# The shift and scale vectors of an adaLN layer: made block by block, or two row blocks in one run

## The chip, the cores and the metric

The kernel runs on one core of a Trainium2 chip. The metric is the time of one execution on the device in microseconds (us). The five engines of the core that matter here are TensorE (PE; its weight loads are shown as PEld), VectorE (DVE), ScalarE (ACT), GpSimd (POOL) and SyncE (SP), whose queue issues nearly all transfers.

## What is computed

One layer of a hybrid diffusion backbone on 640 tokens (128 of context, 512 latent) of width 1024. Each row is normalised and modulated, goes through one wide input projection into attention, a gated linear recurrence and Fourier mixing, and comes back through one output projection. Only the head of the layer is touched by the change:

```
mod_ctx = silu(c_ctx) @ w_ada + b_ada          # context tokens
mod_lat = silu(c) @ w_ada + b_ada              # latent tokens
shift, scale, gate = split(mod, 3)
h = rmsnorm(x, g_pre) * (1 + scale) + shift
proj = h @ w_in
```

`w_ada` is 1024 x 3072 in fp32, so the two thirds that make shift and scale are 8 MB. The latent and the context tokens have vectors of their own, so each entry is needed for two conditions.

## The kernel before

The 1024 channels are cut into KT = 8 row blocks of 128. Tokens lie on the free axis after a transpose: `hT[0]` and `hT[1]` (the high and the low part of h, 128 x 8 x 640 each) are the operands of every input projection. A projection is three matmuls for each block k, each half u of 320 tokens (`mm3`, line 208: high x high, high x low, low x high).

**The loading phase** is `start_stream` (line 242). It issues the loads of x, then for each k two 128 x 1024 blocks of weights (`wss`, 512 KB each, scale and shift of the 128 channels of block k), EARLY = 3 blocks ahead, and for the first two k also a block of `win`. The loads stand in one chain on SP's queue. All x tiles are multiplied by their 1/rms in `scale_x`. Then, for each k:

- `mod_cols` (line 192) makes a raw vector: eight matmuls for each of the two weight blocks, in four groups of 32 output partitions that are added up later. They write two quarters of a PSUM buffer `pm`.
- VectorE copies the 128 x 256 partial sums into `row` (line 264), PE transposes them back into `pm` (line 268), VectorE sums the four groups (line 270) and makes G = (sum + bias + 1) * g_pre in two instructions (lines 271, 272) and the shift in one (line 273).
- `modulated` (line 231): PE transposes four x tiles of block k into a PSUM buffer `px` and the context tile into the last quarter of `pm`; ScalarE makes h from them with G as scale and the shift as bias (line 235 for the 512 latent tokens, line 237 for the 128 of context); VectorE cuts h into `hT[0]` and `hT[1]` (lines 238, 239).

As soon as h of a block is there, `zf_stream` (line 281) adds 12 matmuls of the first two projection blocks to four accumulators `zf_acc` (line 206), which it holds for the whole phase; behind it `fill` (line 956) brings the next projection, `zb0`, from the event "h4" on. After the last block ScalarE runs `gate` (line 319) on the four accumulators, and these come free.

**What sets the order.** `Order` (line 39) runs the streams as generators with rough due times (`od.now`, `LAT`), and so fixes the order in which instructions are written. A planner then goes through them with times of its own and lays down the queue of every engine: an instruction that was written earlier goes first when it is ready by the planner's times. On the chip each queue is worked off in that order. PSUM has eight buffers: five of tag "b" and three of tag "f" (`WB`, line 27). `zf_acc` takes three "f" and one "b"; `pm`, `px` and the first half of `zb0` take "b"; the second half of `zb0` takes an "f".

Of the kernel before, what the change touches and what calls it, by code (L numbers as in the profile page):

```python
# [9 lines left out]
F32 = mybir.dt.float32  # L10
F32R = mybir.dt.float32r
U32 = mybir.dt.uint32
ACT = mybir.ActivationFunctionType
ALU = mybir.AluOpType
AX = mybir.AxisListType
PSUM = bass.MemoryType.PSUM

P = 128
D = 1024
KT = 8  # L20
NT = 640
# [7 lines left out]
EARLY = 3  # L29
# [42 lines left out]
def mixer_kernel(ctx: ExitStack, tc: tile.TileContext, A, O):  # L72
    nc = tc.nc
    sc, ve, gp, te, sy = nc.scalar, nc.vector, nc.gpsimd, nc.tensor, nc.sync
# [5 lines left out]
    sp = ctx.enter_context(tc.tile_pool(name="sp", bufs=WB["s"]))  # L80
    ps = ctx.enter_context(tc.tile_pool(name="ps", bufs=8, space=PSUM))

    od = Order()
# [3 lines left out]
    def nm(s):  # L87
        n_[0] += 1
        return f"{s}_{n_[0]}"

    def T(cols=NT, dt=F32, tag=""):
        return tp.tile([P, NT], dt, tag="t", name=nm("t" + tag))[:, :cols]

    def PE_():
        return tp.tile([P, 512], F32, tag="pe", name=nm("pe"), bufs=WB["pe"])

    def S(cols):
        if cols <= 16:
            return sp.tile([P, 16], F32, tag="s", name=nm("s"))[:, :cols]
        return sp.tile([P, 320], F32, tag="m", name=nm("m"), bufs=WB["m"])[:, :cols]  # L100
# [4 lines left out]
    def PB(tag="b"):  # L105
        return ps.tile([P, 512], F32, tag=tag, name=nm("pb"), bufs=WB["p" + tag])
# [3 lines left out]
    def mm(out, lhsT, rhs, start=True, stop=True):  # L110
        n, m = rhs.free_size(), lhsT.free_size()
        od.now += 1e-3 * (n * 0.4167 * 4 if rhs.dtype == F32 else max(n * 0.4167, m * 0.83)) + 2e-3
        return te.matmul(out, lhsT, rhs, start=start, stop=stop).ins  # L113

    def follow(chain, ins):

        if chain:
            tc.add_manual_dep(ins, chain[-1].name, mybir.DependencyInfo(mybir.DependencyClass.NoSync,
                                                                        mybir.DependencyReason.DATA), reason="turns")
        chain.append(ins)  # L120

    def tr(out, src):
        od.now += 0.107
        last_tr[0] = te.transpose(out, src, ident).ins  # L124

    def split(src, hi, lo, hi_eng=None, lo_eng=None):
        (sc.copy if hi_eng is None else hi_eng.tensor_copy)(hi, src)  # L127
        (ve if lo_eng is None else lo_eng).tensor_sub(lo, src, hi.bitcast(F32))  # L128
# [5 lines left out]
    def const(name, shape, dt=F32, dma=gp.dma_start):  # L134
        t = cp.tile([P, *shape], dt, tag=name, name=name)
        if name in A:
            dma(t, A[name])
        return t
# [3 lines left out]
    bss = const("bss", [KT, 2])  # L142
    gpre = const("gpre", [KT])
# [22 lines left out]
    csil = const("csil", [KT, 32])  # L166
# [5 lines left out]
    def load_raw(src, tag, shape=(KT, P)):  # L172
        t = (tp if tag == "vs" else wp).tile([P, *shape], F32, tag=tag, name=nm(tag), bufs=WB[tag])
        with tc.issue_after(wdma[-1]) if wdma else ExitStack():
            wdma.append(sy.dma_start(t, src).ins)
        return t

    def split_w(raw, lo_eng=None, shape=(KT, P), tags=("hi", "lo")):
        hi, lo = [wp.tile([P, *shape], F32R, tag=t, name=nm(t), bufs=WB[t]) for t in tags]
        split(raw, hi, lo, lo_eng=lo_eng)  # L180
        return hi, lo
# [7 lines left out]
        with tc.issue_after(wdma[-1]) if wdma else ExitStack():  # L189
            sy.dma_start(t, src)  # L190

    def mod_cols(out, w):

        t = od.now
        for k in range(KT):
            o = out[32 * (k % 4):32 * (k % 4) + 32, :]
            mm(o, csil[:, k, :], w[:, k, :], start=(k < 4), stop=(k >= 4))
        od.now = t + 0.45

    shift, G, rstd = const("shift", [KT, 2]), const("G", [KT, 2]), const("rstd", [5])  # L200
    hT = [big.tile([P, KT, NT], F32R, tag=f"hT{j}", name=f"hT{j}") for j in range(2)]
    xa, xb = [T(tag="xa") for _ in range(5)], [T(384, tag="xb") for _ in range(5)]

    def xcols(i, k):
        return (xa[i] if k < 5 else xb[i])[:, k % 5 * P:k % 5 * P + P]
    zf_w, zf_acc = [], [[PB("f"), PB("f")], [PB("f"), PB()]]
# [8 lines left out]
    def load_x():  # L215
        for i in range(5):
            load(xa[i], A["x"][i * P:(i + 1) * P, 0:NT])
            load(xb[i], A["x"][i * P:(i + 1) * P, NT:D])

    def scale_x():  # L220
        for i in range(5):
            ss2 = S(2)
            sc.activation(T(), xa[i], ACT.Square, accum_out=ss2[:, 0:1])
            ve.tensor_tensor_reduce(PE_()[:, 0:384], xb[i], xb[i], 1.0, 0.0, op0=ALU.mult, op1=ALU.add,
                                    accum_out=ss2[:, 1:2])
            ve.tensor_add(rstd[:, i:i + 1], ss2[:, 0:1], ss2[:, 1:2])
            rsqrt_mean(rstd[:, i:i + 1], D)
            ve.tensor_scalar(xa[i], xa[i], rstd[:, i:i + 1], 0.0, op0=ALU.mult, op1=ALU.add)
            ve.tensor_scalar(xb[i], xb[i], rstd[:, i:i + 1], 0.0, op0=ALU.mult, op1=ALU.add)

    def modulated(k, pm):
        h, px = T(), PB()
        for i in range(1, 5):
            tr(px[:, (i - 1) * P:i * P], xcols(i, k))
        sc.activation(h[:, P:NT], px, ACT.Identity, bias=shift[:, k, 1:2], scale=G[:, k, 1:2])
        tr(pm[:, 384:512], xcols(0, k))
        sc.activation(h[:, 0:P], pm[:, 384:512], ACT.Identity, bias=shift[:, k, 0:1], scale=G[:, k, 0:1])
        ve.tensor_copy(hT[0][:, k, :], h)
        ve.tensor_sub(hT[1][:, k, :], h, hT[0][:, k, :].bitcast(F32))
        od.set(f"h{k}", LAT["h"])  # L240

    def start_stream():
        load_x()
        raws, zraw = [], []

        def loads(k):
            for u in range(2):
                raws.append(load_raw(A["wss"][2 * k + u], RAW[2 * k + u]))
            if k < 2:
                zraw.append(load_raw(A["win"][k], "raw"))  # L250

        for k in range(EARLY):
            loads(k)
        scale_x()
        od.now = 11.0
        for k in range(KT):
            if k + EARLY < KT:
                loads(k + EARLY)
            row = sp.tile([P, 256], F32, tag="AC", name=nm("row"), bufs=2)
            pm = PB()  # L260
            for u in range(2):
                mod_cols(pm[:, u * P:(u + 1) * P], raws[2 * k + u])
            yield 0
            ve.tensor_copy(row, pm[:, 0:256])
            yield LAT["row"]

            for u in range(2):
                tr(pm[:, u * P:(u + 1) * P], row[:, u * P:(u + 1) * P])
            pt = S(4)
            ve.reduce_sum(pt, pm[:, 0:256].rearrange("p (u g r) -> p u r g", u=2, r=32)[:, :, 0:2, :], axis=AX.X)  # L270
            ve.tensor_scalar(G[:, k, :], pt[:, 0:2], bss[:, k, 0:1], 1.0, op0=ALU.add, op1=ALU.add)
            ve.tensor_scalar_mul(G[:, k, :], G[:, k, :], gpre[:, k:k + 1])  # L272
            ve.tensor_scalar_add(shift[:, k, :], pt[:, 2:4], bss[:, k, 1:2])
            modulated(k, pm)
            if k < 2:
                zf_w.append(split_w(zraw[k]))
            if k == 1:
                od.set("zw", 0.0)
            yield max(0.0, 13.5 + 2.7 * (k + 1) - od.now)

    def zf_stream():
        yield "zw"
# [9 lines left out]
        od.set("zf", 0.0)  # L292

    od.add(start_stream())
    od.add(zf_stream())

# [832 lines left out]
```

## Time and profile before

| | us |
|---|---|
| median of three runs | 436.22 (436.12 to 437.0) |
| the profiled execution | 437.11 |
| its span, from the first to the last instruction | 435.3 |
| PE busy | 411.3 |
| VectorE busy | 303.5 |
| ScalarE busy | 205.8 |

The busy time of PE has the ends of its matmuls modelled, so a busy PE is not one at its peak: the time from one start to the next is what counts. The chain of waits is followed back from the last instruction: at each step to what released it, or to the instruction before it on its engine. All times in the rows below count from the start of the span.

### The profile page before, as it was taken

How to read it: one execution, taken by the hardware profiler on the slowest of the kernel's cores; microseconds unless marked ns; L12 is line 12 of the kernel's file. 1: busy time of each engine (PE TensorE's matmuls, PEld its weight loads, DVE VectorE, ACT ScalarE, POOL GpSimd, SP SyncE). 2: the span in 40 equal slices, each digit the busy share in tenths (PEclk: the TensorE clock that was granted, in tenths of full speed). 3: DMA queues.
4: the chain of work that ended last, by engine and by line, in shares of the span. 5: the costliest groups of instructions: out<-in, count | busy, mean ns of one | idle time of the engine just before them, and what ended most of it. 6: DMA issues, size and time to landing. Idle time of an engine off the chain costs nothing.

```text
span 435.3 us, 8309 instructions
## 1 busy us (share of the span) xinstructions
PE 411.3 (94%) x3176; PEld 372.7 (86%) x3176; DVE 303.5 (70%) x866; ACT 205.8 (47%) x546; POOL 7.4 (2%) x23
## 2 busy tenths in 40 slices
PE   0699999999998999999999999999999999999994
PEld 0488899999988998999899889889898988988884
DVE  2775479999986866885597658885768928670174
ACT  6434467565341526654444444753556643350161
POOL 2000000000020100000000000000000000000000
PEclk9999999999999999999999999999999999999998
DMA  7996153211302021122021413245134302481023
GB/s 236 412 407 229 49 158 114 74 45 50 88 20 76 10 62 48 56 97 74 32 68 60 145 50 104 98 147 163 51 119 150 96 0 66 140 291 48 0 105 139
DMA packets 19528, 47.62 MB, mean 109 GB/s; under 512 B 3184, under 2 KB 6912, under 8 KB 19488
## 3 DMA queue, kind: packets, MB, share of 16 engines
q1 hardware_dynamic: 19376, 46.94, 32.0%
q8 instruction: 25, 0.41, 0.4%
q0 software_dynamic: 112, 0.14, 0.3%
q14 instruction: 15, 0.12, 0.1%
HBM read 43.80 MB, written 3.28 MB: 108 GB/s over the span
## 4 chain that ended last, share of the span: by engine, by line
PE 90%; DVE 3%; DMA 3%; ACT 1%; issue 1%; SPq 0%; DVEq 0%; ACTq 0%
PE pb L113 84%; PE pb L124 7%; DMA vs<-wss 2%; DMA txa<-x 1%; DVE AL L450 1%; DVE t L524 1%; DVE AL L487 0%; ACT L679 0%; DVE t L951 0%; ACT pe L680 0%; DVE t L467 0%; DVE t L466 0%; DVE AC L450 0%; DVE t L468 0%; SPq L190 0%
## 5 line engine op out<-in xcount | busy, mean ns | idle before, releaser
L113 PE MATMUL pb<-hT,hi 128*128 128x320 f32 x896 | 208.7, 317 | 2.5 <-DVE vs L128 1.5
L113 PEld LDWEIGHTS pb<-hT,hi 128*128 128x128 f32 x896 | 148.7, 188 | 9.0 <-issue 3.3
L113 PE MATMUL pb<-hT,lo 128*128 128x320 f32 x448 | 139.1, 312 | 0.0
L113 PEld LDWEIGHTS pb<-hT,lo 128*128 128x128 f32 x448 | 84.0, 188 | 1.3 <-DVE G L272 0.2
L128 DVE TENSOR_TENSOR lo<-raw,hi 128x1024 fp32r<-128x1024 f32 x35 | 42.8, 1223 | 18.7 <-ACT hi L127 18.5
L127 ACT CAST hi<-raw 128x1024 fp32r<-128x1024 f32 x35 | 36.8, 1050 | 28.4 <-PE pb L113 17.5
L113 PE MATMUL pb<-t,t 64*128 64x128 f32 (+2 forms) x414 | 42.9, 291 | 0.4 <-DVE AL L450 0.4
L113 PEld LDWEIGHTS pb<-t,t 64*128 64x128 f32 (+1 forms) x414 | 36.0, 188 | 4.7 <-issue 0.7
L127 ACT CAST pT<-pb 128x256 fp32r<-128x256 f32 x64 | 23.5, 373 | 22.3 <-DVE pT L128 11.1
L113 PE MATMUL pb<-hi,mh 128*128 128x512 f32 (+1 forms) x108 | 30.8, 375 | 0.0
L128 DVE TENSOR_TENSOR pT<-pb,pT 128x256 fp32r<-128x256 f32 x64 | 26.5, 419 | 1.7 <-ACT pT L127 1.5
L679 ACT ACTIVATE pe<-pb,s 128x256 f32<-128x256 f32 x32 | 15.3, 478 | 17.5 <-DVE s L678 8.4
L113 PEld LDWEIGHTS pb<-hi,mh 128*128 128x128 f32 x108 | 19.6, 188 | 3.7 <-DVE mh L128 0.3
L113 PE MATMUL pb<-pT,mh 128*128 128x512 f32 (+1 forms) x102 | 21.9, 364 | 0.0
L124 PE MATMUL pb<-ident,pe 128*128 128x128 f32 x136 | 21.0, 274 | 0.5 <-ACT pe L680 0.5
L113 PEld LDWEIGHTS pb<-pT,mh 128*128 128x128 f32 x102 | 17.7, 189 | 3.1
L113 PE MATMUL pb<-lo,mh 128*128 128x512 f32 (+1 forms) x54 | 19.5, 375 | 0.0
L934 ACT ACTIVATE t<-pb 128x512 f32<-128x512 f32 (+1 forms) x11 | 6.1, 552 | 26.9 <-PE pb L113 26.7
L690 DVE TENSOR_TENSOR o<-pb,o 64x512 f32<-64x512 f32 (+1 forms) x16 | 7.8, 486 | 15.5 <-ACT o L689 15.4
L124 PEld LDWEIGHTS pb<-ident,pe 128*128 128x128 f32 x136 | 16.5, 140 | 1.7 <-ACT pe L680 0.7
L450 DVE COPY_PREDICATED AL<-masks,pb 128x512 f32<-128x512 uint32 x24 | 16.6, 742 | 1.7 <-PE pb L113 1.6
L113 PE MATMUL pb<-pT,vs 128*128 128x256 f32 (+1 forms) x96 | 17.0, 320 | 0.0
(205 smaller groups left out, 635.3 us busy)
## 6 DMA issues: line engine op xcount, KB each, us to landing
raw<-win SPq DMA_DIRECT2D x30, 512.0 KB, 3.5
pT<-wss SPq DMA_DIRECT2D x12, 512.0 KB, 10.3
raw<-wg SPq DMA_DIRECT2D x8, 512.0 KB, 3.6
raw<-wout SPq DMA_DIRECT2D x8, 512.0 KB, 3.6
t<-x SPq DMA_DIRECT2D x10, 256.0 KB, 5.4
o_y<-t SPq DMA_DIRECT2D x9, 256.0 KB, 2.2
vs<-wss SPq DMA_DIRECT2D x4, 512.0 KB, 9.5
tbl<-tbl SPq DMA_DIRECT2D x4, 512.0 KB, 3.5
```

Of the source, the lines that this page charges most:

```text
L113: return te.matmul(out, lhsT, rhs, start=start, stop=stop).ins
L124: last_tr[0] = te.transpose(out, src, ident).ins
L127: (sc.copy if hi_eng is None else hi_eng.tensor_copy)(hi, src)
L128: (ve if lo_eng is None else lo_eng).tensor_sub(lo, src, hi.bitcast(F32))
L450: ve.copy_predicated(out, mk.to_broadcast([P, i1 - i0, P]), src)
L524: ve.scalar_tensor_tensor(sall[r, cdst], sall[r, cs], Td[r, ip:ip + 1], pst[r, cdst], op0=ALU.mult, op1=ALU.add)
L679: sc.activation(pe[:, 256:512], ss[:, 256:512], ACT.Exp, bias=m[:, 1:2], accum_out=m[:, 3:4])
L690: ve.tensor_add(out, src[r, :], out)
L934: sc.activation(T(512)[:, cs], po[:, 0:cs.stop - cs.start], ACT.Square, accum_out=ssb[:, j:j + 1])
```

## The change

The eight row blocks are no longer handled one by one but in five groups: block 0 alone, blocks 1 and 2, 3 and 4, 5 and 6, and block 7 alone. In a group of two the four weight blocks are multiplied one after the other into the four quarters of one `pm` (a dependency on PE's own order, `follow`, keeps the matmuls in sequence), with one copy of 512 columns, four transposes, one sum, one instruction that adds the biases of both shift and scale for all vectors, and one that makes G from it. Shift and scale stand in one tile `ss_`. `row` is taken from the tag "pe" in place of "AC". The context tile of a block is no longer transposed into a free quarter of `pm` but into the quarter of `pm` that held its own vector, which the sum has read by then. The order in which weight blocks are loaded stays; the loads of two blocks are written together, ahead of the group.

```diff
-    def mod_cols(out, w):
-
-        t = od.now
+    def mod_cols(out, w, chain=None):
+
+        t, chain = od.now, [] if chain is None else chain
         for k in range(KT):
             o = out[32 * (k % 4):32 * (k % 4) + 32, :]
-            mm(o, csil[:, k, :], w[:, k, :], start=(k < 4), stop=(k >= 4))
+            follow(chain, mm(o, csil[:, k, :], w[:, k, :], start=(k < 4), stop=(k >= 4)))
         od.now = t + 0.45
...
-    def modulated(k, pm):
+    def modulated(k, pc):
...
-        sc.activation(h[:, P:NT], px, ACT.Identity, bias=shift[:, k, 1:2], scale=G[:, k, 1:2])
-        tr(pm[:, 384:512], xcols(0, k))
-        sc.activation(h[:, 0:P], pm[:, 384:512], ACT.Identity, bias=shift[:, k, 0:1], scale=G[:, k, 0:1])
+        sc.activation(h[:, P:NT], px, ACT.Identity, bias=ss_[:, k, 1, 1:2], scale=G[:, k, 1:2])
+        tr(pc, xcols(0, k))
+        sc.activation(h[:, 0:P], pc, ACT.Identity, bias=ss_[:, k, 1, 0:1], scale=G[:, k, 0:1])
...
-        for k in range(KT):
-            if k + EARLY < KT:
-                loads(k + EARLY)
-            row = sp.tile([P, 256], F32, tag="AC", name=nm("row"), bufs=2)
-            pm = PB()
-            for u in range(2):
-                mod_cols(pm[:, u * P:(u + 1) * P], raws[2 * k + u])
+
+        for k0, k1 in ((0, 1), (1, 3), (3, 5), (5, 7), (7, 8)):
+            for k in range(k0 + EARLY, min(k1 + EARLY, KT)):
+                loads(k)
+            n = 2 * (k1 - k0)
+            row, pm, chain = PE_()[:, 0:n * P], PB(), []
+            for u in range(n):
+                mod_cols(pm[:, u * P:(u + 1) * P], raws[2 * k0 + u], chain)
             yield 0
-            ve.tensor_copy(row, pm[:, 0:256])
+            ve.tensor_copy(row, pm[:, 0:n * P])
             yield LAT["row"]
 
-            for u in range(2):
+            for u in range(n):
                 tr(pm[:, u * P:(u + 1) * P], row[:, u * P:(u + 1) * P])
-            pt = S(4)
-            ve.reduce_sum(pt, pm[:, 0:256].rearrange("p (u g r) -> p u r g", u=2, r=32)[:, :, 0:2, :], axis=AX.X)
-            ve.tensor_scalar(G[:, k, :], pt[:, 0:2], bss[:, k, 0:1], 1.0, op0=ALU.add, op1=ALU.add)
-            ve.tensor_scalar_mul(G[:, k, :], G[:, k, :], gpre[:, k:k + 1])
-            ve.tensor_scalar_add(shift[:, k, :], pt[:, 2:4], bss[:, k, 1:2])
-            modulated(k, pm)
-            if k < 2:
-                zf_w.append(split_w(zraw[k]))
-            if k == 1:
-                od.set("zw", 0.0)
-            yield max(0.0, 13.5 + 2.7 * (k + 1) - od.now)
+            pt, sv = S(2 * n), ss_[:, k0:k1]
+            ve.reduce_sum(pt, pm[:, 0:n * P].rearrange("p (u g r) -> p u r g", u=n, r=32)[:, :, 0:2, :], axis=AX.X)
+            ve.tensor_add(sv.rearrange("p k w r -> p (k w) r"), pt.rearrange("p (u r) -> p u r", r=2),
+                          bss[:, k0:k1, :].rearrange("p k w -> p (k w)").unsqueeze(2).to_broadcast([P, n, 2]))
+            ve.scalar_tensor_tensor(G[:, k0:k1, :], sv[:, :, 0, :], 1.0,
+                                    gpre[:, k0:k1].unsqueeze(2).to_broadcast([P, k1 - k0, 2]), op0=ALU.add, op1=ALU.mult)
+            for k in range(k0, k1):
+                modulated(k, pm[:, (k - k0) * P:(k - k0 + 1) * P])
+                if k < 2:
+                    zf_w.append(split_w(zraw[k]))
+                if k == 1:
+                    od.set("zw", 0.0)
+                yield 0
+            yield max(0.0, 13.5 + 2.7 * k1 - od.now)
```

## Rows read from the trace of the kernel before

**Rows 1.** The page: PE's busy time, and the chain that ended last by engine.

```profile
PE 411.3 (94%) x3176; PEld 372.7 (86%) x3176; DVE 303.5 (70%) x866; ACT 205.8 (47%) x546; POOL 7.4 (2%) x23
...
PE 90%; DVE 3%; DMA 3%; ACT 1%; issue 1%; SPq 0%; DVEq 0%; ACTq 0%
```

**Rows 2.** Busy time by stretch: stretch, its length, each engine; clock, DMA share, GB/s.

```profile
14.00:22.80 8.80, 8.06 (x79) 4.89 (x79) 6.22 (x18) 3.51 (x5) 0.00 (x0) 1.00 1.03 411
22.80:52.60 29.80, 29.80 (x354) 26.74 (x354) 17.79 (x52) 9.98 (x16) 0.00 (x0) 1.00 0.61 236
...
54.00:120.00 66.00, 66.00 (x570) 62.65 (x571) 60.95 (x139) 38.90 (x91) 0.00 (x0) 1.00 0.29 89
```

**Rows 3.** The chain of waits, 14 to 56 us: start, length, what.

```profile
25.03 1.36 PE pb L113 x20
...
30.58 1.01 PE pb L113 x32
31.59 0.59 PE pb L124 x4
32.17 1.76 PE pb L113 x12
33.94 0.33 PE pb L124 x3
...
51.95 1.18 issue
```

**Rows 4.** Order of time on PE and PEld: start, length, instruction, records, idle time before.

```profile
25.25 0.38 PEld L113 LDWEIGHTS pb<-pT,csil 128*32 128x32 f32 x16 [0.19 <-issue]
25.26 0.64 PE L113 MATMUL pb<-pT,csil 128*32 128x128 f32 x16
...
26.45 0.20 PEld L124 LDWEIGHTS pb<-ident,row 128*128 128x128 f32 x2 [0.22 <-DVE row L264]
...
26.82 0.81 PEld L113 LDWEIGHTS pb<-pT,csil 128*32 128x32 f32 x32 [0.17 <-ACT t L235]
...
31.52 0.42 PEld L124 LDWEIGHTS pb<-ident,txa 128*128 128x128 f32 x4 [0.20 <-issue]
...
42.04 1.08 PE L113 MATMUL pb<-pT,csil 128*32 128x128 f32 x32
```

**Rows 5.** Order of time on ScalarE, same columns.

```profile
25.81 0.78 ACT L235 ACTIVATE t<-pb,shift,G 128x512 f32<-128x512 f32 x1 [3.40 <-DVE G L272]
...
40.17 0.78 ACT L235 ACTIVATE t<-pb,shift,G 128x512 f32<-128x512 f32 x1 [3.54 <-DVE G L272]
...
47.26 0.78 ACT L235 ACTIVATE t<-pb,shift,G 128x512 f32<-128x512 f32 x1 [2.78 <-DVE G L272]
49.16 0.46 ACT L237 ACTIVATE t<-pb,shift,G 128x128 f32<-128x128 f32 x1 [1.12 <-PE pb L124]
51.84 1.28 ACT L323 ACT_TABLE_LOAD   x1 [2.22 <-PE pb L113]
53.13 0.44 ACT L323 ACTIVATE t<-pb 128x320 f32<-128x320 f32 x1
53.47 0.43 ACT L324 ACTIVATE t<-pb 128x320 f32<-128x320 f32 x1
```

**Rows 6.** Transfers of `wss`: duration of the issues, first and last start; time to landing.

```profile
L175 SPq DMA_DIRECT2D pT<-wss x12: 327/327/423, 8.3 to 26.0; - x12
...
DMA to landing us min/median/max: 6.6/10.2/10.9
```

**Rows 7.** Groups on VectorE by shape: count, busy us, mean ns, idle before.

```profile
L264 DVE COPY row<-pb 128x256 f32<-128x256 f32 x8 | 3.4, 422 | 1.0 <-PE pb L113 1.0
L271 DVE TENSOR_SCALAR G<-s,bss 128x2 f32<-128x2 f32 x8 | 1.8, 228 | 0.2
L270 DVE TENSOR_REDUCE s<-pb 128x4 f32<-128x16 f32 x8 | 1.4, 173 | 6.4 <-PE pb L124 6.4
...
L939 DVE TENSOR_TENSOR t<-pb,t 128x512 f32<-128x512 f32 x7 | 4.7, 685 | 0.3 <-ACT t L934 0.3
```

More of the change, by code (lines that the diff above doesn't have):

```diff
@@ L190, in load @@
             sy.dma_start(t, src)
-    def mod_cols(out, w):
-        t = od.now
+    def mod_cols(out, w, chain=None):
+        t, chain = od.now, [] if chain is None else chain
         for k in range(KT):
             o = out[32 * (k % 4):32 * (k % 4) + 32, :]
-            mm(o, csil[:, k, :], w[:, k, :], start=(k < 4), stop=(k >= 4))
+            follow(chain, mm(o, csil[:, k, :], w[:, k, :], start=(k < 4), stop=(k >= 4)))
         od.now = t + 0.45
-    shift, G, rstd = const("shift", [KT, 2]), const("G", [KT, 2]), const("rstd", [5])
+    ss_, G, rstd = const("ss", [KT, 2, 2]), const("G", [KT, 2]), const("rstd", [5])
     hT = [big.tile([P, KT, NT], F32R, tag=f"hT{j}", name=f"hT{j}") for j in range(2)]
```

## The prediction

> **What bounds the kernel now.** I read the page first, then the busy time by stretch, then the loading phase in the chain of waits and in each engine's order of time. TensorE is busy for 94% of the span and carries 90% of the chain [rows 1], so a time is gained only where PE's own queue gets shorter or loses a gap. By stretch [rows 2] PE is busy 29.80 of the 29.80 us from 22.8 to 52.6 us, where the vectors are made, and 66.00 of 66.00 us after 54; VectorE has 17.79 us of work in the first of these, ScalarE 9.98. Between them lies one gap: the chain stands at "issue" from 51.95 us for 1.18 us [rows 3], which is the table load and the first gate on ScalarE [rows 5].
>
> Two more things are to be seen. The vectors aren't late because of loads: the last block of `wss` is issued at 26.0 us, no landing took over 10.9 us [rows 6], so it is there by 36.9, while its matmuls start at 42.04 [rows 4]. And a run of vector matmuls is started when ScalarE lets a PSUM buffer go: the run at 26.82 us waits for the activation of line 235 [rows 4], which ends at 25.81 + 0.78 = 26.59 [rows 5]; the one at 42.04 starts 1.1 us behind the activation that ends at 40.95. Of the five buffers of tag "b", `zf_acc` holds one, so `pm` and `px` of two blocks fill the other four, and the vectors of block k+2 wait for a buffer of block k.
>
> **What the work on PE costs.** A weight block is 16 records (8 matmuls in two passes). In one run 16 records take 0.64 us and 32 take 1.08 [rows 4], so 16 more cost 0.44. On the chain a lone run costs more: the 20 records at 25.03 us are the 16 of the run at 25.26 and four matmuls on `hT`, which take 1.76 / 12 = 0.147 us each, so the run holds the chain for 1.36 - 0.59 = 0.77 us, 0.33 above its 0.44. A pair holds it for 1.01, and the four transposes behind it take 0.59 where four in a row of others take 4 x 0.33 / 3 = 0.44 [rows 3]: 1.16 in all, 0.28 above its 0.88. So each change between vectors and other work costs 0.28 to 0.33 us; a run joined to another gains 0.28, a pair cut in two loses 2 x 0.33 - 0.28 = 0.38. The loads of weights show the same as 0.19 to 0.20 us of idle time ahead of a run and behind it [rows 4].
>
> **The change, part by part.**
>
> Removed on VectorE: eight groups of copy, sum and three small instructions (0.42 + 0.17 + 3 x 0.23 [rows 7], 1.28 us each, 10.2 us). Added: five groups. Two keep a width of 256 and lose one small instruction, with 1.05 us each. Three have a copy of 512 columns, which the trace lacks; the nearest row, a product of 512 columns from PSUM, takes 0.69 us [rows 7], its lower bound is the 0.42 of 256 columns, and I take 0.69. With a sum of 0.17 to 0.21 and two small ones of 0.23 that is some 1.34 us, so 2 x 1.05 + 3 x 1.34 = 6.1 us in all. VectorE loses 4.1 us that PE does not wait for: PE has 29.8 us of work in that stretch and VectorE 17.79. On the path this is nothing, with one exception: at 26.45 us the transposes of `row` waited 0.22 us for the copy [rows 4]. If that wait stays it is 0.27 us longer for the wider copy, at three places at most 0.8 us; if it goes, 0.22 us is gained. I take 0.
>
> The number of matmuls and transposes on PE is the same. What can change is how often it switches. From 22.8 us on there are eight runs now: two lone ones, of which the one at 25.26 is shown, four pairs, of which those at 26.82, 30.58 and 42.04 are shown, and one pair that is cut in two [rows 3, 4]. Four blocks asked for at once give at best runs of 64, five in all (the lone ones are still paced by landings): 3 x 0.28 = 0.9 us gained. But a pair's `pm` gets its buffer earlier (the buffer of block 0 goes to blocks 3 and 4 in the place of block 2), and then the landings pace the runs: 0.52 MB at the 411 GB/s of this stretch [rows 2] is, as an estimate, a block every 1.3 us, and a planner that puts each block on PE as it lands makes twelve lone runs: 4 x 0.38 = 1.5 us lost. Between these ends I take eight runs, no change, since the first two lone runs and the last pair have no reason to change and for the others both pulls exist.
>
> The wait for the pair: block 1's vectors wait for block 2's weights. Queued behind on PE are the four transposes of `row`, then everything of h1 and h2. Two blocks more at 1.3 us each, less the 1 us or so that PE is behind the landings, put block 1's `zf` matmuls 1 to 2 us later than now. In PE's queue meanwhile stand the rest of `zf` for block 0, the transposes of block 2, and the vectors of blocks 3 and 4, 4 x 0.44 us and their changes, which are now free to run; that is 2.5 to 3.5 us of work, so I cost the wait at 0; without this cover it is up to 2 us once, and later none of it returns, as PE has no slack behind it.
>
> Issued on SP: the weight loads of two blocks are asked for together; the order of the blocks on the queue stays as it was, and they land 5 us before use [rows 4, 6]. Nothing.
>
> The gap at 51.95 us: PE's next accumulator (second half of `zb0`) is one that `zf_acc` holds until ScalarE has loaded a table (1.28 us) and run two gate activations, 51.84 to 53.90 us [rows 5]. h7 is late today (its two activations are at 47.26 and 49.16 us [rows 5], 4 and 6 us behind its vectors at 43.1), so `zf` of block 7 ends PE's list. With buffers free sooner h7 is ready well before the end, `zf` of block 7 runs ahead of the last three matmuls of `zb0` and of whatever else of `zb0` is left, and part of the 2.1 us on ScalarE lies under them. 3 to 6 matmuls are 0.44 to 0.88 us. I take 0.6 us gained; the ends are 0 and the 1.18 us of the row.
>
> Sum: 0 + 0 + 0 + 0 - 0.6 = -0.6 us, from 437.11 us of the profiled execution (span 435.3 and 1.8 around it) 436.5, and from the median of the runs, which stands 0.89 us lower, 436.22 - 0.6 = **435.6 us**. What 0.2% is here, about 0.87 us, is what a measurement of this kernel can tell from no change.
>
> **The rivals.** *Merged runs* (faster). All groups from block 3 on run as one: -0.9 for the runs, -0.2 for the wait on the copy, -0.9 for most of the gap: 434.2 us. For it: from block 3 on the pairs of today are hardly cut [rows 3, 4]. Against it: the runs that are paced by landings today are lone ones.
>
> *The planner gives back what was joined* (no change). Twelve lone runs cost 1.5 us and the gap gives 0.9: 436.8 us at the far end, 436.2 with two runs less.
>
> *The shared bank* (slower). Today the transposes of the first token tile go to a free quarter of `pm`, which is that block's own. After, the second block's transpose writes the bank from which ScalarE still has to read the first's. ScalarE takes 0.78 + 0.46 us for the two activations of a block [rows 5]. Where PE's queue has the second transpose within 1.24 us behind the first (some 8 matmuls), PE stands until that read is done, and all behind it too: up to 1.24 us at three pairs, 3.7 us; half of it, less the gap's 0.6, gives 436.22 + 1.8 - 0.6 = 437.4, the whole 439.3 us. For it: PE's order is fixed beforehand, and ScalarE waits for a late transpose of PE today (1.12 us ahead of line 237 at 49.16 us [rows 5]), so the planner's times and the chip's aren't the same. Against it: 12 matmuls of `zf` per block are there to lie between.
> The Trainium skill speaks for this rival (PSUM — Partial Sum Buffer, Terms): TensorE writing and ScalarE or VectorE reading one bank in the same quadrant at once is an error, so the two must be kept apart although they touch other columns. The trace of before can't settle it: in it each block's transpose into `pm` comes after the block's sum anyway.
>
> **How the numbers follow.** The forecast (eight runs, half the gap) has 0.45, with a range of its own from 435.0 to 436.4: a quarter of it lies beyond 0.87 us. Merged runs 0.25, all faster. Given back 0.12, three quarters of it within 0.2%. Shared bank 0.18, nearly all slower. So faster 0.45 x 0.26 + 0.25 = 0.37; same 0.33 + 0.09 + 0.01 = 0.43; slower 0.03 + 0.17 = 0.20. The range leaves out the better half of the merged runs and the far half of the shared bank: 433.9 to 437.6 us.
>
> **What would show it.** Right: PE full from 22.8 us to the gap; seven to nine runs of vectors in that time; the gap between the load phase and the long stretch down from 1.2 to about 0.6 us; VectorE with 4 us less. Wrong towards faster: runs of 64 in PE's order. Towards slower: PE's waits name the activation of line 237 or the copy of `row`, or the runs are lone ones up to block 7. The forecast fails as a whole if the order after 54 us changes, since PE has no slack there either.

## The result, and the profile after

The changed kernel takes 438.61 us in the median (438.31 to 438.91), the kernel before beside it 436.31; the ratio is 1.0050 with an interval from 1.0032 to 1.0067. It is slower by 2.3 us, where 435.6 was forecast and 437.6 was the end of the range. Two more comparisons with the kernel before gave 1.0047 (1.0035 to 1.0060) and 1.0045 (1.0032 to 1.0057), that is 2.3 and 1.7 us in medians. The profiled execution took 438.91 us with a span of 437.1, against 437.11 and 435.3.

First the busy times of the page, which answer to [rows 1], then the stretches of [rows 2] in the same columns:

```profile
PE 413.5 (95%) x3176; PEld 373.7 (85%) x3176; DVE 301.1 (69%) x846; ACT 205.2 (47%) x546; POOL 7.4 (2%) x23
```

```profile
14.00:22.80 8.80, 8.59 (x94) 6.00 (x95) 5.73 (x16) 3.62 (x5) 0.00 (x0) 1.00 1.03 410
22.80:52.60 29.80, 29.71 (x335) 25.22 (x327) 15.09 (x33) 8.94 (x15) 0.00 (x0) 1.00 0.61 233
```

VectorE has lost 2.7 us in the second stretch and nobody has gained by it: PE is as full as before. From the first vector matmul to the last one ahead of the gap PE runs 432 records in either kernel, and it takes longer over them in the changed one (the two stretches together hold 433 of its records before and 429 after). So PE does the same work at a slower pace. The order of PE's queue behind the loading phase is the same in both kernels, and the 381 us from the end of the gap to the end of the span are the same in every kernel below within 0.4 us. What is to be explained lies between the first vector matmul and the first matmul behind the gap: 14.54 to 53.95 us before (39.41 us), 14.07 to 55.39 after (41.32 us).

PE's order of time, as in [rows 4]:

```profile
24.07 0.64 PE L113 MATMUL pb<-pT,csil 128*32 128x128 f32 x16
...
26.01 0.65 PE L113 MATMUL pb<-pT,csil 128*32 128x128 f32 x16
...
27.17 0.65 PE L113 MATMUL pb<-pT,csil 128*32 128x128 f32 x16
...
28.00 0.64 PE L113 MATMUL pb<-vs,csil 128*32 128x128 f32 x16
...
29.43 0.64 PE L113 MATMUL pb<-pT,csil 128*32 128x128 f32 x16
...
32.40 0.65 PE L113 MATMUL pb<-pT,csil 128*32 128x128 f32 x16
...
34.49 0.65 PE L113 MATMUL pb<-pT,csil 128*32 128x128 f32 x16
```

A run is a stretch of PE's queue with vector matmuls only. Seven lone runs of 16 records follow one another where the kernel before has two lone ones and then pairs of 32, one of them cut in two. Counted in PE's queue there are 15 runs of vectors in the whole phase instead of 12, or 11 instead of 8 from 22.8 us on; no group of four runs as one. The waits of PE's weight loads between 15 and 57 us (for what; total us, times, longest), first before, then after, say what a run costs:

```profile
PEld pb L113 <- issue: 2.1, 10, 0.3
PEld pb L124 <- issue: 1.6, 6, 0.4
```

```profile
PEld pb L113 <- issue: 3.5, 16, 0.3
PEld pb L124 <- issue: 1.6, 6, 0.4
PEld pb L113 <- ACT t L328: 1.3, 1, 1.3
PEld pb L124 <- DVE pe L265: 0.4, 1, 0.4
...
PEld pb L124 <- ACT t L235: 0.4, 1, 0.4
PEld pb L124 <- DVE ss L272: 0.2, 1, 0.2
```

"Issue" is the idle time at a change between vectors and other work; it is 1.4 us more, in six more pieces, two for each run more. The 1.3 us for line 328 are the gap, which the kernel before has too; the other waits for another engine are short.

### The profile page after: what moved, and what is told of

It reads as the page before. It is cut to its first block, busy times and chain, and to the rows that moved or that the text cites. A ratio compares the mean times of both kernels' runs of the same rounds, so it can differ in the third digit from the quotient of the medians.

```text
span 437.1 us, 8289 instructions
## 1 busy us (share of the span) xinstructions
PE 413.5 (95%) x3176; PEld 373.7 (85%) x3176; DVE 301.1 (69%) x846; ACT 205.2 (47%) x546; POOL 7.4 (2%) x23
## 4 chain that ended last, share of the span: by engine, by line
PE 90%; DVE 3%; DMA 3%; ACT 1%; issue 1%; SPq 0%; DVEq 0%; ACTq 0%
PE pb L113 84%; PE pb L124 7%; DMA vs<-wss 1%; DMA txa<-x 1%; DVE AL L454 1%; DVE t L528 1%; DVE AL L491 0%; ACT L683 0%; DVE t L955 0%; ACT pe L684 0%; DVE t L471 0%; DVE t L470 0%; DVE AC L454 0%; DVE t L472 0%; SPq L190 0%
## 5 line engine op out<-in xcount | busy, mean ns | idle before, releaser
L124 PE MATMUL pb<-ident,pe 128*128 128x128 f32 x152 | 23.9, 277 | 0.6 <-ACT pe L684 0.5
L124 PEld LDWEIGHTS pb<-ident,pe 128*128 128x128 f32 x152 | 18.5, 141 | 2.4 <-ACT pe L684 0.7
L113 PE MATMUL pb<-vs,csil 128*32 128x128 f32 x64 | 3.9, 350 | 14.1 <-DMA vs<-wss 14.1
## 6 DMA issues: line engine op xcount, KB each, us to landing
pT<-wss SPq DMA_DIRECT2D x12, 512.0 KB, 10.2
```

## The theories

*The switches*: three more runs of vectors cost 0.3 to 0.5 us each and make up the loss. *The wait of the first pair*: the vectors of block 1 wait until those of block 2 are through, and h1 and h2 (h of blocks 1 and 2) come late with nothing to fill the time. *The clock*: PE works at its lower level at the head of the phase (16 vector records take 1.08 us there and 0.64 us later), and the change makes that stretch cost more.

## Experiments

Each is timed against the kernel before on the same chip. The numbers of runs of vectors are counted in PE's queue over the whole phase: 12 before, 15 after.

### Runs cut and joined

Four versions change the number of runs. The kernel before with the second weight block of blocks 3 to 7 held apart from the first by that block's own transposes (16 runs):

```diff
             for u in range(2):
-                mod_cols(pm[:, u * P:(u + 1) * P], raws[2 * k + u])
+                mod_cols(pm[:, u * P:(u + 1) * P], raws[2 * k + u], chain)
+                if u == 0 and k >= 3:
+                    px = PB()
+                    for i in range(1, 5):
+                        tr(px[:, (i - 1) * P:i * P], xcols(i, k))
+                        follow(chain, last_tr[0])
```

the changed kernel with eight single blocks (14 runs), with blocks 1 and 2 single (15 runs), and with the weight block that lands last taken first from block 3 on (10 runs):

```diff
-        for k0, k1 in ((0, 1), (1, 3), (3, 5), (5, 7), (7, 8)):
+        for k0, k1 in tuple((k, k + 1) for k in range(KT)):
```

```diff
-        for k0, k1 in ((0, 1), (1, 3), (3, 5), (5, 7), (7, 8)):
+        for k0, k1 in ((0, 1), (1, 2), (2, 3), (3, 5), (5, 7), (7, 8)):
```

```diff
-            for u in range(n):
+            for u in (reversed(range(n)) if k0 >= 3 else range(n)):
                 mod_cols(pm[:, u * P:(u + 1) * P], raws[2 * k0 + u], chain)
```

> The kernel before with one thing changed: from block 3 on the four transposes of x are put between the two weight blocks, by an order on PE, so a pair of vector runs is cut in two. PE's queue has 16 runs of vector matmuls in the loading phase, where before has 12 and after has 15. Theory S (switches: each run more costs PE 0.28 to 0.38 us): 436.3 + 4 x 0.33 = 437.6 us. Theory W (the wait for the pair: block 1's vectors wait for block 2's weights): no pair waits here, 436.3 us. Theory C (TensorE's records get short later): as W, 436.3.

> The kernel after with eight groups of one block: all of the rewriting stays (fewer small instructions on VectorE, the context tile in the vector's own quarter, the order within a group), only the joining of two blocks is undone. PE's queue has 14 runs. Theory S: 436.3 + 2 x 0.33 = 437.0 us. Theory W: nothing waits for a second block, 436.3 us or less by the 0.1 to 0.3 us that the shorter work on VectorE gives.

> The kernel after with blocks 1 and 2 each alone, and the pairs 3 and 4, 5 and 6 kept. PE's queue has 15 runs, as many as after. Theory S: as after less nothing, some 437.3 to 438.6 us. Theory W: the wait of the first pair, about 1 to 1.5 us in the trace of after, is gone: 437.0 us, and what stays belongs to the two later pairs.

> The kernel after, but from block 3 on the weight blocks of a group are multiplied in reverse order, so a run starts only when the last of its blocks has landed and the others lie ready. PE's queue has 10 runs in place of 15 and still the pairs. Theory S: 438.6 - 5 x 0.33 = 437.0 us. Theory W: the pairs wait as long as before or longer, 438.6 us or more.

Measured: 437.94, 437.60, 438.23 and 440.57 us, the kernel before 436.93; ratios 1.0020 (1.0011 to 1.0030), 1.0012 (1.0003 to 1.0021), 1.0029 (1.0018 to 1.0040) and 1.0077 (1.0063 to 1.0091). The first is the cleanest: nothing of the change is in it, only cuts (with them comes an order on PE within a block, and `px` is taken a little earlier), and it loses 1.0 us. Its weight loads show the cuts as the changed kernel does:

```profile
PEld pb L113 <- issue: 3.5, 16, 0.3
PEld pb L124 <- issue: 1.8, 7, 0.4
```

That is 5.3 us of idle time where the kernel before has 3.7, and its phase is 1.5 us longer.

The fourth is the surprise: joined runs, and the worst time of all up to here. A stretch of its trace in steps of 2 us (stretch, length, each engine's busy time, granted clock, DMA share, GB/s), PE's weight loads and PE's order of time:

```profile
26.00:28.00 2.00, 0.72 (x5) 0.30 (x3) 0.52 (x3) 0.94 (x2) 0.00 (x0) 1.00 1.01 401
28.00:30.00 2.00, 1.56 (x13) 1.04 (x17) 1.72 (x3) 1.21 (x3) 0.00 (x0) 0.83 1.03 410
30.00:32.00 2.00, 2.00 (x44) 1.84 (x40) 0.83 (x1) 0.00 (x0) 0.00 (x0) 0.50 1.02 408
32.00:34.00 2.00, 2.00 (x37) 1.73 (x28) 0.69 (x1) 0.00 (x0) 0.00 (x0) 0.81 1.03 412
```

```profile
28.24 0.14 PEld L124 LDWEIGHTS pb<-ident,txa 128*128 128x128 f32 x1 [1.42 <-ACT t L237]
```

```profile
29.67 1.08 PE L113 MATMUL pb<-pT,csil 128*32 128x128 f32 x16
...
31.38 1.72 PE L113 MATMUL pb<-pT,csil 128*32 128x128 f32 x32
```

The vectors of blocks 3 and 4 now wait for the block that lands last, so they no longer fill the time in which h1 and h2 are made. PE is busy for 0.72 of 2 us, and the context transpose of block 2 waits 1.42 us until ScalarE has read that of block 1 from the same buffer (this is the rival of the shared bank, and the only place where its full wait shows). This wait sets nothing by itself: behind it PE's next matmuls wait for h1 until 28.77 us, and the chain goes through h1. Then the granted clock falls to 0.50 and the records get longer (16 of vectors in 1.08 us). The cover that the prediction counted on for the pair's wait is real: this is what its absence costs, in this kernel together with the slow records behind it.

### Which joined pair costs, and what the cover is worth

```diff
-        for k0, k1 in ((0, 1), (1, 3), (3, 5), (5, 7), (7, 8)):
+        for k0, k1 in ((0, 1), (1, 2), (2, 3), (3, 4), (4, 6), (6, 8)):
...
-            for u in range(n):
+            for u in (reversed(range(n)) if k0 >= 3 else range(n)):
```

(pairs 4/5 and 6/7 only, last landed first: 9 runs); blocks 1 and 2 single, with the last landed first (9 runs); only the pair 1/2 joined (13 runs):

```diff
-        for k0, k1 in ((0, 1), (1, 3), (3, 5), (5, 7), (7, 8)):
+        for k0, k1 in ((0, 1), (1, 3), (3, 4), (4, 5), (5, 6), (6, 7), (7, 8)):
```

and the kernel before with the second weight block first from block 3 on (11 runs).

> The kernel after with other groups: blocks 0 to 3 each alone, then 4 and 5, 6 and 7; from block 4 on the weight blocks of a group are taken in reverse order, so the run starts when its last block is there. PE's queue has 9 runs of vectors, two of them of four blocks in one piece. It has pairs, and fewer runs than before (12). Theory S (0.39 us for a run, from the three kernels with 14, 15 and 16 runs): phase 39.4 - 3 x 0.39 = 38.2 us, time 1.2 us below before. Theory W (a pair costs by its wait): two pairs' waits, at or above the time of before. Theory P (what costs is that the vectors are made in pairs, whatever the order): between before and after, 1 us above before.

> As the kernel with blocks 1 and 2 each alone and pairs 3 and 4, 5 and 6, which had 15 runs, but from block 3 on the weight blocks of a group are taken in reverse order: 9 runs. Against that kernel only the order of the blocks within a run differs. Theory S: 6 x 0.39 = 2.3 us less than it, 1 us below before. Theory W: the wait for the last block of the pair is the same or longer: no gain on it.

> The kernel after with only the pair of blocks 1 and 2; all others alone. 13 runs. Theory S: 0.4 us above before. Theory W: the wait of the first pair without the vectors of blocks 3 and 4 as one group behind it: PE's records show idle time between 26 and 30 us, and the time is 0.4 + up to 1 us above before.

> The kernel before, in which from block 3 on the second weight block of a row block is multiplied first. 11 runs in place of 12, as the run that was cut in two is now whole. Theory S: 0.4 us below before, near what can be measured. Theories W and P: no change.

Measured, against 436.51 us: 437.00 (1.0014, 1.0005 to 1.0023), 436.81 (1.0004, 0.9995 to 1.0013), 439.26 (1.0074, 1.0060 to 1.0088) and 436.78 (1.0011, 1.0001 to 1.0020). Of the joins, that of blocks 1 and 2 is the expensive one when it stands alone, with 2.7 us, of which its one run more explains some 0.3. Its stretches have no full one between 18 and 30 us, so PE has run out of work:

```profile
18.00:22.00 4.00, 3.15 (x55) 2.29 (x57) 1.78 (x5) 2.18 (x3) 0.00 (x0) 1.00 1.03 410
22.00:26.00 4.00, 3.18 (x48) 2.33 (x44) 2.58 (x4) 0.00 (x0) 0.00 (x0) 1.00 1.03 405
26.00:30.00 4.00, 3.65 (x48) 2.49 (x41) 2.25 (x9) 2.27 (x5) 0.00 (x0) 1.00 1.02 406
```

The version with blocks 1 and 2 single and nine runs joins the rest of what the change meant to join, and stands within 0.3 us of the kernel before, not below it. Three runs less than before should be worth 0.9 us; its trace shows where they go. Waits of PE's weight loads between 15 and 57 us:

```profile
PEld pb L113 <- issue: 1.2, 6, 0.3
PEld pb L113 <- DVE hT L238: 1.2, 2, 0.9
PEld pb L124 <- issue: 1.1, 4, 0.4
PEld pb L124 <- DVE s L271: 1.0, 2, 0.5
PEld pb L124 <- DVE pe L265: 0.7, 2, 0.4
PEld pb L113 <- DVE hT L239: 0.4, 2, 0.3
...
PEld pb L113 <- ACT t L328: 0.4, 1, 0.4
```

The changes are down from 3.7 to 2.3 us, and the gap is smaller too: the wait for line 328 is 0.4 us where the kernel before and the changed one have 1.3. ScalarE is done with h of block 7 at 46.7 us here:

```profile
45.89 0.81 ACT L237 ACTIVATE t<-pb,ss,G 128x128 f32<-128x128 f32 x2 [1.01 <-PE pb L124]
```

Against these gains PE now stands for the sum of a group (0.5 us twice, not at all before) and for the h of its blocks (1.2 and 0.4 us, where it was 0.9 before): a group of two has its sums and its h later and at once. This execution is the fastest of its kernel, with short records from 19.78 us on and a phase 0.6 us shorter than before; in the kernel's second profile, with long ones until 22 us, the phase is as long as before (39.34 us).

Fewer runs did not pay in the other versions either. Pairs 4/5 and 6/7 with nine runs are 0.5 us slower than the kernel before. The kernel before with one run less is 0.3 us slower and not 0.4 faster; in its trace PE's weight loads wait 0.6 us for h at 50.76 us, which they don't in the trace of before.

### PE kept busy ahead of the vectors

The records are long at the head of the phase. To have PE at work earlier, 24 products of the identity with itself, whose result is not used, stand ahead of the vectors: in the kernel before, the changed kernel, the kernel before with the second block first, and the version of nine runs.

```diff
+NW = 24
...
         scale_x()
+        pw = PB()
+        for _ in range(NW):
+            te.matmul(pw[:, 0:P], ident, ident, start=True, stop=True)
         od.now = 11.0
```

> The kernel before with 24 matmuls of the identity with itself ahead of the first vectors (their result is not used), so PE works from some 4 us on and its records should be short (0.64 us for 16 vector records in place of 1.08) from the first run on. 12 runs of vectors. Theory C (the loss of the kernel after comes from long records that last longer): this and the next kernel stand equal. Theory S and W: the next one stays 1.6 to 2.3 us above this one. Against the kernel before: PE's runs until 22 us are paced by landings in part, so 1 to 2 us less.

> The kernel after with the same 24 matmuls of the identity. 16 runs of vectors. Theory C: equal to the kernel before with these matmuls. Theories S and W: 4 runs more at 0.39 us, 1.6 us, and the wait of the first pair, 0 to 0.7 us, above it.

> The kernel before with the 24 matmuls and, from block 3 on, the second weight block of a row block first. 11 runs. Theory S: 0 to 0.4 us below the kernel before with the 24 matmuls.

> The kernel after with blocks 1 and 2 alone, pairs 3 and 4, 5 and 6, the last landed weight block first from block 3 on, and the 24 matmuls. 9 runs. Theory S alone: 1.2 us below the kernel before with the 24 matmuls. Without them this grouping stood at the time of before although it has 3 runs less, as PE waits for the sums and h of its pairs; if PE's work is done sooner these waits get longer: at the time of the kernel before with the 24 matmuls.

Measured, against 436.80 us: 436.12 (0.9984, 0.9973 to 0.9995), 439.24 (1.0064, 1.0048 to 1.0080), 437.13 (1.0008, 0.9998 to 1.0018) and 436.41 (0.9995, 0.9986 to 1.0005). The slow stretch was moved, not removed. PE's order of time and a stretch of the first version:

```profile
13.57 0.65 PE L114 MATMUL pb<-vs,csil 128*32 128x128 f32 x16 [1.91 <-DMA vs<-wss]
...
17.32 0.64 PE L114 MATMUL pb<-pT,csil 128*32 128x128 f32 x16 [0.29 <-DMA pT<-wss]
...
19.68 1.08 PE L114 MATMUL pb<-pT,csil 128*32 128x128 f32 x16
```

```profile
20.00:22.00 2.00, 2.00 (x21) 1.56 (x14) 1.17 (x2) 0.89 (x1) 0.00 (x0) 0.50 1.04 408
```

The vectors are short at first and long later, at a granted clock of 0.50, after PE had stood for 1.91 us ahead of them and four times for 0.3 to 0.4 us between them. In the second version the granted clock is 0.50 from 16 to 22 us, in the third from 14 to 22 us. So the clock isn't tested by this: the edit did not keep the records short through the head. The changed kernel loses more to its counterpart with the same edit (3.1 us, with 16 runs of vectors against 12) than without it, and the version with 11 runs is 1.0 us slower than that with 12, where up to 0.4 less was expected. The first version is the fastest here, 0.7 us below the kernel before, which is less than the 0.2% that a measurement can tell with ease.

### Side by side: is it the first pair?

The changed kernel and the one with blocks 1 and 2 single have 15 runs each and differ in that join alone.

> The changed kernel itself, beside a version that differs from it in one thing only, blocks 1 and 2 single. If three more runs of vectors and the wait of the first pair share the loss, it stands 2.0 to 2.6 us above the kernel before, and 0.7 to 1.3 us above the version beside it. If the runs of vectors are the whole loss, the two are within 0.3 us of each other, since both have 15 runs. If the wait of the first pair is the whole loss, it stands over 1.8 us above the version beside it.

> Blocks 1 and 2 single, the others as in the changed kernel; 15 runs of vectors as there. By runs and wait together 1.0 to 1.5 us above the kernel before and 0.7 to 1.3 us below the changed kernel; by runs alone the time of the changed kernel within 0.3 us; by the wait of the first pair alone the time of the kernel before within 0.4 us.

Measured: 438.61 us both, the kernel before 436.27; ratios 1.0047 (1.0035 to 1.0060) and 1.0049 (1.0036 to 1.0063). In the changed kernel the join of the first pair costs nothing that shows within some 0.8 us. The profiled execution of the changed kernel differs from the first one in its clock. Its order of time on PE:

```profile
17.33 0.64 PE L113 MATMUL pb<-pT,csil 128*32 128x128 f32 x16
...
19.04 0.64 PE L113 MATMUL pb<-pT,csil 128*32 128x128 f32 x16
21.05 0.65 PE L113 MATMUL pb<-vs,csil 128*32 128x128 f32 x16 [1.37 <-DMA vs<-wss]
22.51 0.85 PE L113 MATMUL pb<-hT,hi 128*128 128x320 f32 x4 [0.82 <-DVE hT L238]
```

Here the records are short from 16.93 us on, where the first profile has them long until 23.16. PE gets to the third of the pair's four weight blocks before it has landed and stands for 1.37 us, and then 0.82 us for h of block 0. The second wait isn't the pair's. The kernel before with its late pairs cut has it too, in an execution whose records are short early (line 240 there makes the high part of h):

```profile
20.88 0.82 PE L113 MATMUL pb<-hT,hi 128*128 128x320 f32 x3 [0.90 <-DVE hT L240]
```

From the first vector to the first matmul behind the gap it is 13.46 to 54.73 us, 41.27 us, against 41.32 with the long records. So there are two ways to the same time: with a slow PE the waits are hidden, with a quick one they take what the pace had won.

### Side by side: runs of vectors

> The changed kernel, 15 runs of vectors, as the measure for the three beside it on the same chip. 1.9 to 2.5 us above the kernel before.

> The kernel before with its late pairs cut, 16 runs of vectors and nothing else of the change. If the number of runs sets the time, it is level with the changed kernel or up to 0.8 us above it. If something else in the change costs as much as the runs, it is at least 0.8 us below the changed kernel although it has one run more.

> The changed code with eight single blocks, 14 runs. By the number of runs 0.2 to 0.8 us below the changed kernel and 1.2 to 2.0 us above the kernel before. If joining blocks costs something beside the runs, over 1.0 us below the changed kernel.

> Blocks 1 and 2 single, from block 3 on the block that lands last first; 9 runs. By the number of runs 1.5 to 3 us below the changed kernel. If the joined copies and sums themselves cost the time, within 0.8 us of it.

| on one chip | runs of vectors | us | ratio (interval) |
|---|---|---|---|
| kernel before | 12 | 436.63 | |
| nine runs, last landed first | 9 | 436.88 | 1.0004 (0.9995 to 1.0013) |
| eight single blocks | 14 | 437.34 | 1.0025 (1.0014 to 1.0036) |
| changed kernel | 15 | 438.31 | 1.0045 (1.0032 to 1.0057) |
| kernel before, pairs cut | 16 | 438.02 | 1.0034 (1.0022 to 1.0046) |

Cutting alone makes 1.4 of the changed kernel's 1.7 us on this chip, and 1.0 on the other. By the two comparisons of each, a cut costs 0.25 and 0.35 us with the pairs cut (four cuts), 0.34 and 0.36 with single blocks (two more runs), and 0.24 us lie between 15 and nine runs (1.43 / 6, which has the first pair's join, a smaller gap and more waits in it too). Three more runs at 0.25 to 0.36 us are then 0.8 to 1.1 us: about half of the 1.7 to 2.3 us, shown by the kernel with cuts alone, which has nothing else of the change. The claim that the number of runs orders all times does not hold in full: the kernel with 16 runs is 0.3 us below that with 15, with intervals that overlap.

The single blocks, 0.97 us below the changed kernel, are just at the edge of what had been set as the sign of a cost beside the runs.

**What stays open** is the other part, 0.6 to 1.6 us. Where it stands can be read from PE's order of time. Each of the 432 records takes the time up to the start of the next, and for records of one kind in one place that time is the same everywhere at the short length, so what goes beyond it can be sorted into changes, long records (those at the lower level) and waits. By this sum, which is rough to 0.1 us, the 1.91 us between the changed kernel's first profile and the kernel before are 1.1 us at changes, 0.8 in long records and nothing in waits. In its second profile they are again 1.1 at changes, with 1.0 less in long records and 1.7 more in waits; in the third 1.1 and 0.9 more in long records, and 0.2 less in waits. So the open part stands in the head of the phase, before 24 us. Long records and waits come together to 5.9 to 6.0 us in the three profiles of the changed kernel. In the seven profiles of the kernel before, of that with pairs cut, of single blocks and of blocks 1 and 2 single they come to 4.7 to 5.8. That points to the first pair, but the two kernels side by side don't show it.

The clock is the other candidate: the changed kernel has five long weight blocks in two of its three profiles (two in the third), the kernel before four in its one. A version without that pair (pairs 4/5 and 6/7) has five as well, the last of them this:

```profile
22.83 1.08 PE L113 MATMUL pb<-vs,csil 128*32 128x128 f32 x16
```

The two profiles of the kernel with blocks 1 and 2 single show how much this differs between executions of one kernel. In their chains, the same four projection matmuls with one run of vectors, start, length, what, first on one chip, then on another:

```profile
21.12 1.76 PE pb L113 x20
```

```profile
22.39 2.37 PE pb L113 x20
```

The 0.6 us between them is all of the difference of their phases (40.79 and 41.40 us). Whether the change makes the clock rise later, or these executions happened to, can't be told from three profiles. The same spread carries the first pair's join: nothing side by side, 0.4 us (1.0047 against the mean of 1.0029 and 1.0049) across chips.

## Why the prediction was wrong, point by point

**What bounds the kernel: right.** PE is full and its order decides; VectorE's time buys nothing. Its groups by shape in the changed kernel:

```profile
L265 DVE COPY pe<-pb 128x512 f32<-128x512 f32 x3 | 2.1, 688 | 0.9 <-PE pb L113 0.9
L271 DVE TENSOR_REDUCE s<-pb 128x8 f32<-128x32 f32 x3 | 0.6, 192 | 3.8 <-PE pb L124 3.8
L272 DVE TENSOR_TENSOR ss<-s,bss 128x8 f32<-128x8 f32 x3 | 0.5, 164 | 0.1
```

The wide copy takes 0.69 us, as taken from the nearest row; the small instructions 0.16 where 0.23 was taken. The copies, sums and small instructions of the vectors made 10.2 us before and make 5.4 now: 4.8 are saved where 4.1 was forecast (the page's total falls by 2.4), worth nothing. Waits for the copy are one of 0.4 us where two made 0.7 before: the predicted 0, within its bounds.

**The number of runs: the step that failed.** The prediction set its range from five runs to twelve (from 22.8 us on) and took eight, "no change, since the first two lone runs and the last pair have no reason to change and for the others both pulls exist". Eleven came, three more at 0.25 to 0.36 us each: 0.8 to 1.1 us where the sum has 0. Both pulls did exist: in blocks 6 and 7 the vectors stand nearly together, cut by a single transpose, and from the second weight block of block 2 to the end of block 5 each is alone, close to the sign that the prediction had named for slower. The reason had been written down as the rival that gives back what was joined: with a buffer to be had earlier, the landings pace the runs. They do so by the planner's times: the queue is laid out beforehand, and on the chip no wait of PE in the first profile names one of these loads behind the first vector. The versions that ask for the last landed block first show this cause, since with that alone the runs fall from 15 to ten, and from 15 to nine with blocks 1 and 2 single. The price of a run, 0.28 to 0.38 us, was right (0.25 to 0.36 measured). The mistake was to take the middle between two ends as if it were the likeliest, and then to give it no cost.

**The gap: failed, and with it the whole gain of the sum.** 0.6 us were to come from h7 being ready early. The gap is as long as in [rows 3], and ScalarE waits for PE's context transposes as it did for one in [rows 5]:

```profile
53.39 1.18 issue
```

```profile
38.98 0.46 ACT L237 ACTIVATE t<-pb,ss,G 128x128 f32<-128x128 f32 x1 [1.67 <-PE pb L124]
...
45.50 0.46 ACT L237 ACTIVATE t<-pb,ss,G 128x128 f32<-128x128 f32 x1 [1.47 <-PE pb L124]
...
49.57 0.46 ACT L237 ACTIVATE t<-pb,ss,G 128x128 f32<-128x128 f32 x1 [1.28 <-PE pb L124]
```

In all it waits for them four times in either kernel, 15 to 57 us, first before, then after:

```profile
ACT t L237 <- PE pb L124: 3.3, 4, 1.1
```

```profile
ACT t L237 <- PE pb L124: 5.0, 4, 1.7
```

The last vectors are done at 42.7 us (43.1 before) and h7 at 50 us: buffers were free sooner, but the late transposes in PE's fixed order are what holds h7, and the change doesn't bring those forward. The prediction had the row and read it only as a reason for the bank rival. The step behind it was right: where h7 is ready early, at 46.7 us in the version with blocks 1 and 2 single and nine runs, the wait ahead of the accumulator falls from 1.3 to 0.4 us, the upper end of the 0.44 to 0.88 us that were counted.

**The wait of the pair: near in its size without cover, half right on the cover.** "Without this cover it is up to 2 us once" is some 2.4 us with that pair alone, after 0.3 for its run more. In the changed kernel the wait for h1 and h2 is covered by the vectors of blocks 3 and 4, as predicted. What was not foreseen comes earlier: in the execution whose records are short early PE stands 1.37 us for the pair's third block, and in the others that is hidden because the records are long until some 23 us. That is luck and not the cover that was named. The prediction took the rate of landings and the speed of PE as fixed; the wait depends on both.

**The loads: right** in that the first profile of the changed kernel waits for no load behind the first vector; but in the execution with early short records the pair waits for a landing at 21.05 us, a wait that the trace of before doesn't have at that place.

**The rivals.** Merged runs did not come, and the nine runs that an edit forced gained nothing over the kernel before: the -0.9 us for the runs and the 0.9 us of the gap were both there in the traces, and were eaten by 1.0 us of waits for sums and 0.7 more for h. The planner that gives back was the right mechanism at 0.12, and too cheap: it was to give 436.2 to 436.8 us because the gap's 0.9 us were set against it. Without the gap, eleven runs by the prediction's own price are 436.22 + 3 x 0.38 = 437.4 us. Shared bank: not in the changed kernel (the one wait of a transpose for ScalarE is 0.4 us and names line 235), only where the cover was taken away, and there PE had to wait longer for h1 anyway.

**The range** ended at 437.6 us, below the 438.3 to 438.6 measured: it left room for the one cost or the other, and the runs at 1.1 us with the gap not gained and another 0.6 to 1.6 us of waits and clock are more than either.

## What to carry to other kernels

Joining instructions on an engine that isn't the bound paid nothing here in itself; what decided was how the join changed the order on the engine that is. Before giving a middle value between two orders, find out what would let the better one happen: here the operands' landings by the planner's times, not the free buffers, decided whether matmuls of one kind stand together. And a join makes what stands behind it late and due at once, so what it saved in switches on PE returned as waits for the sums and for h, where no other work stood there.

## What was not expected of the hardware

- The records at the head of the phase are as long as elsewhere at a granted clock of 0.50 (16 vector records take 1.08 us, against 0.64), while the clock's column shows 1.00 there. By their length PE is at the lower of its two levels. When they turn short differs from one execution to the next of one kernel: by 16.93 us in one of the changed kernel, not before 23.16 in another.
- The column does show a fall once PE's records have been short and PE has then been idle: 0.50 from 30 to 32 us with the last landed block first (PE busy 0.72 of 2 us in 26 to 28), and from 20 to 22 us with early work on PE.
- Executions of one kernel differ by up to 1.3 us in when the first weights land (first vector at 13.61 and 14.88 us in two profiles of one kernel, on two chips), as much as a good part of the effect; spans of single profiles were no measure here, and the medians of versions on one chip were needed.
